# Raw weight blocks of Strassen units kept by rows and loaded in two row halves, instead of by column halves

## The chip, the cores and the metric

The kernel runs on one core of one Trainium2 chip. The metric is the device time of one execution, in microseconds (us), as the median over several runs. Five engines take part: TensorE (PE in the profile, its weight loads PEld), VectorE (DVE), ScalarE (ACT), GpSimd (POOL) and SyncE (SP), which here mainly starts transfers between device memory and on-chip memory. Each engine works through its own instructions in the order in which they stand in the built program, and waits at the first one whose inputs or whose place are not ready.

## The reference

One sequence of 512 tokens, with 16 learned positions ahead of it (528 rows), runs through two layers of width 1024: gated linear attention (GLA) and then differential softmax attention. Each layer is a norm, one wide input projection, the attention branch, a SiLU gate and an output projection. The changed lines serve the input projections alone:

```python
def gla_branch(xn, w_in, w_gate_up, b_gate, gnorm, w_out):
    proj = xn @ w_in                      # [528, 1024] @ [1024, 6160]
    q, k, v, z, g_lr = jnp.split(proj, ...)
...
def diff_branch(xn, w_in, lam_vecs, gnorm, w_out, rel_table, lambda_init):
    proj = xn @ w_in                      # [528, 1024] @ [1024, 8192]
    q, k, v, z = jnp.split(proj, 4, axis=-1)
```

All of it is float32.

## The kernel before

**Projections as Strassen units.** Float32 products are made of three passes over numbers split in a high and a low part (`split`: ACT writes the high part, line L269; DVE subtracts it from the source to get the low part, L270). On top of that, most projections are done by a Strassen-like scheme with seven products instead of eight. A *unit* is 256 columns of a weight matrix with all 1024 rows: a 2 by 2 arrangement of blocks, each of 512 rows and 128 columns. The kernel numbers them 0 to 3: 0 and 1 are the upper and the lower 512 rows of the first 128 columns, 2 and 3 the same of the second 128 columns. On chip a block is 128 partitions by 512 numbers (four groups of 128 rows, side by side). There are 45 such loads in the program; 41 of them are Strassen units (`want_unit`) and 4, the first ones of the GLA layer, are used without sums (`want_plain`).

**From raw block to operand.** `load_blocks` (L281) reserves one of two `raw` buffers of 1 MB each and starts two transfers from SP (L285), one for each column half: blocks 0 and 1, then blocks 2 and 3. Each transfer is 512 KB in 1024 pieces of 512 bytes. A unit then needs six parts, made in this order by `Weights.make_one`:

- `a11`: block 0 split (128x512);
- `sum`: three DVE additions (L337, helper `add`): `sum[1]` = block 2 + block 3, `sum[0]` = `sum[1]` + block 0, and block 2 += block 0 in place;
- `s21`: `sum` split (128x1024, tiles `wh` and `wl`);
- `a12`: block 1 split;
- `s43`: the *outer add* (`raw<-raw,sum`, a fourth addition), block 1 += `sum[0]` in place, and then blocks 1 and 2 split together (128x1024). This split's DVE half, `wl<-raw`, mostly is the last reader of the buffer, and releases it for the load after the next;
- `a22`: block 3 split.

**Orders.** PE's order is written by hand: `Unit.run` yields its products (L402, 128x264 matmuls, into the banks `bx`, `by` and `bv`), and a `Weaver` weaves them between the attention's own matmuls. The orders on DVE and ACT are not written down. The build's scheduler puts an instruction where it expects its inputs and its engine to be free, with some helpers (`partial` at L423, the combining adds `t`, `qs` at L448 to L452) at a raised priority. So a changed dependence between two instructions can change the order of others.

**What else stands around the change in the GLA layer.** For each head, a value block is normalised: ACT sums squares (L1215), DVE scales the sum (L512) and POOL takes a power (L513), ACT multiplies (L1217), PE transposes (L1239), DVE applies the gate (L1241). Output of a unit is evicted by L448 to L452.

Of the kernel before, what the change touches and what calls it, by code (L numbers as in the profile page):

```python
# [11 lines left out]
F32 = mybir.dt.float32  # L12
# [8 lines left out]
P = 128  # L21
# [52 lines left out]
class Weaver:  # L74
# [6 lines left out]
    def add(self, gen, us=0.0):  # L81
        self.queue.append(gen)
        self.left += us
        return gen
# [124 lines left out]
def trunk(ctx, tc, x, meta, g_norm, gla_w_in, gla_w_gate_up, gla_b_gate, gla_gnorm, gla_w_out,  # L209
# [3 lines left out]
    act, dve, pe, pool, sp = nc.scalar, nc.vector, nc.tensor, nc.gpsimd, nc.sync  # L213
# [8 lines left out]
    wp = ctx.enter_context(tc.tile_pool(name="wp", bufs=2))  # L222
# [8 lines left out]
    def T(p, shape, dt, tag, **kw):  # L231
        uid[0] += 1
        return p.tile(shape, dt, tag=tag, name=f"{tag}_{uid[0]}", **kw)
# [29 lines left out]
    def split(hi, lo, src, scale=None, keep=False):  # L263

        if keep:
            act.activation(hi, src, AF.Copy)
            kept.append(lambda: dve.tensor_tensor(lo, src, hi.bitcast(F32), op=ALU.subtract))
        elif scale is None:
            act.activation(hi, src, AF.Copy)  # L269
            dve.tensor_tensor(lo, src, hi.bitcast(F32), op=ALU.subtract)  # L270
        else:
            act.activation(hi, src, AF.Copy, scale=scale)
            dve.scalar_tensor_tensor(lo, src, scale, hi.bitcast(F32), op0=ALU.mult, op1=ALU.subtract)
# [4 lines left out]
        sp.dma_start(t, w[r0:r0 + nk * P, c0:c0 + ncol].rearrange("(k p) c -> p k c", p=P))  # L278
        return t

    def load_blocks(w, c0):  # L281

        t = T(wp, [P, 4, 512], F32, "raw")
        for i in range(2):
            sp.dma_start(t[:, 2 * i:2 * i + 2, :].rearrange("p j (k c) -> p (j k) c", k=4),  # L285
                         w[:, c0 + i * P:c0 + (i + 1) * P].rearrange("(k p) c -> p k c", p=P))
        return t

    W = Weaver()
    behind = W.behind  # L290

    def load(key):
        t = load_w(*key) if len(key) == 4 else load_blocks(*key)
        while behind:
            behind.pop(0)()
        return t

    def w_pair(shape):
        return [T(wp, shape, F32R, tag) for tag in ("wh", "wl")]
# [7 lines left out]
    ws = Weights(lambda *key: load(key), {"pair": 2, "sum": 1, "a11": 1, "a12": 1, "a22": 1})  # L307
# [8 lines left out]
    def behind_gate():  # L316
        st = ExitStack()
        for i in W.gated:
            st.enter_context(tc.issue_after(i.ins))
        return st  # L320

    def block_pair(src, keep=False):
        wh, wl = w_pair([P, 2, 512])
        split(wh, wl, src, keep=keep)
        return [[t[:, i, :] for t in (wh, wl)] for i in range(2)]

    def want_unit(w, c0, calm=False):
        def single(tag, b):
            def fn(raw):
                t = [T(wp, [P, 512], F32R, tag + part, bufs=1) for part in "hl"]  # L330
                with tc.issue_after(W.moved.ins) if calm and b == 0 else ExitStack():
                    split(*t, raw[:, b, :])
                return t
            return Part(tag, fn)

        def add(o, a, b):
            dve.tensor_tensor(o, a, b, op=ALU.add)  # L337

        def sums(raw):
            t = T(wp, [P, 2, 512], F32, "sum", bufs=1)  # L340
            add(t[:, 1, :], raw[:, 2, :], raw[:, 3, :])
            add(t[:, 0, :], t[:, 1, :], raw[:, 0, :])
            add(raw[:, 2, :], raw[:, 2, :], raw[:, 0, :])
            return t

        def outer(raw):
            add(raw[:, 1, :], raw[:, 1, :], su.t[:, 0, :])
            ws.room["sum"] += 1
            return block_pair(raw[:, 1:3, :])

        a11, a12, a22 = single("a11", 0), single("a12", 1), single("a22", 3)
        su = Part("sum", sums)
        s21 = Part("pair", lambda raw: block_pair(su.t))
        s43 = Part("pair", outer)
        ws.want((w, c0), [a11, su, s21, a12, s43, a22])
        return a11, a12, a22, s21, s43

    def want_plain(w, c0, keep=False):

        def first(raw):  # L360
            with behind_gate():
                return block_pair(raw[:, :2, :], keep)

        return ws.want((w, c0), [Part("pair", first),
                                 Part("pair", lambda raw: block_pair(raw[:, 2:, :]))])

    def mm3(ps, a, b, first=True, last=True, **kw):

# [240 lines left out]
    for b in range(5):  # L609
        t0, n = BLK[b]  # L610
        t = T(gp, [P, D], F32, ("qs", "ks")[b - 1]) if b in (1, 2) else {0: z2, 3: v2[0], 4: v2[1]}[b][:, 1, :]
# [5 lines left out]
    sp.dma_start(glr_raw, g_w_in[:, 6144:6160].rearrange("(k p) c -> p k c", p=P))  # L617

    v_first = [want_plain(g_w_in, 2048 + c, c == 0) for c in (0, 256)]
    ws.held = 1  # L620
    ws.fetch()
# [124 lines left out]
    for k0 in range(0, KT, 2):  # L746
        if k0 + 2 < KT:
            scaled_pair(k0 + 2)
        i, ks = k0 // 4, slice(k0 % 4, k0 % 4 + 2)
# [28 lines left out]
    def q_gla_qk(hd, s):  # L778
        c = 256 * hd
        us = [(want_unit if hd else want_plain)(g_w_in, c0) for c0 in (c, 1024 + c)]  # L780

        def factor_of(i, sign, e=None):
# [176 lines left out]
    for k in range(KT):  # L959
        for n in range(2):  # L960
            for i, x in enumerate((X["b11"], b12) if k < 4 else (X["b21"], X["b22"])):
                if k == 0:
                    warm_up((3, 3, 1, 4)[2 * n + i], idle)
                if (k, 2 * n + i) in turns_of:
                    b, half = turns_of[k, 2 * n + i]
# [49 lines left out]
    first = q_gla_qk(0, heads[0])  # L1015
# [395 lines left out]
    for i in range(2):  # L1411
        w = ws.take()
# [354 lines left out]
    for hd in range(D_HEADS):  # L1767
# [6 lines left out]
        keep = {D_HEADS - 1: 0.0, D_HEADS - 2: 22.0}.get(hd, 3.0)  # L1774
# [85 lines left out]
def build(shapes):  # L1860
    import concourse.bacc as bacc

    nc = bacc.Bacc("TRN2", target_bir_lowering=False, num_devices=1, dynamic_dma_scratch_size=512)
    args = [nc.dram_tensor(f"in_{n}_dram", shp, F32, kind="ExternalInput").ap() for n, shp in shapes]
    args.append(nc.dram_tensor("out_0_dram", (1, NR, D), F32, kind="ExternalOutput").ap())
    with tile.TileContext(nc) as tc:
        trunk(tc, *args)
    return nc
# [15 lines left out]
```

## Time and profile before

| what | value |
|---|---|
| median of the runs | 984.81 us (984.6 to 985.19) |
| the profiled execution's own time | 986.58 us |
| span of the profile (first to last instruction) | 984.8 us, granted PE clock 0.997 |
| PE busy | 969.7 us (98%) in 7065 matmuls |
| DVE busy | 777.3 us (79%) in 1584 instructions |
| ACT busy | 615.6 us (63%) in 1306 instructions |
| queue q1 (all plain transfers) | 147504 packets, 89.61 MB, 33.5% of 16 DMA engines |

The span leaves out 1.8 us of the execution's own time, which lie ahead of the first and behind the last instruction. The profiled execution is 1.8 us above the median of the runs. "Busy" says how long an engine had an instruction under way; a row of the timeline has the start, the duration, the engine, the line and the tiles (written tile, arrow, read tiles), and in brackets how long the engine had been idle and what ended that. A releaser given as "DMA raw" is the landing of a weight transfer.

### The profile page before, as it was taken

To read this page: it belongs to the slowest core of one execution; us is meant where nothing else is said; L and a number is where in the kernel's file an instruction comes from. 1 tells how busy PE (TensorE), PEld (TensorE's weight loads), DVE (VectorE), ACT (ScalarE), POOL (GpSimd) and SP (SyncE) were. 2 spreads that over 40 slices of the span, in tenths; PEclk is the share of its full clock that TensorE was granted. 3 is DMA by queue.
4 is the path that set the end of the run, shared out by engine and by line. 5 is a ranking of instruction groups with operands and counts; after the bars stand their busy time and mean duration, and the time that the engine had idled before them with its cause. 6 is when DMAs were issued, how large, how long until landed. Compare 5 with 4: busy or idle time off the path is not lost. (4 is left out here: it accounts for less than half of the span.)

```text
span 984.8 us, 18186 instructions
## 1 busy us (share of the span) xinstructions
PE 969.7 (98%) x7065; PEld 915.2 (93%) x7065; DVE 777.3 (79%) x1584; ACT 615.6 (63%) x1306; POOL 50.7 (5%) x68
## 2 busy tenths in 40 slices
PE   8999999999999999999999999999999999999997
PEld 8999999999999999999999998898998999988896
DVE  7889985987687888556998885877968879677785
ACT  7776755566546666536657675566764667654583
POOL 1000000000000100000000101001010000000001
PEclk9999999999999999999999999999999999999999
DMA  7322223731363322122332524335353351622222
GB/s 194 87 74 74 74 87 127 143 87 44 111 158 87 86 73 76 68 86 87 97 87 77 149 63 137 83 98 135 86 147 86 97 135 49 184 60 81 86 65 86
DMA packets 150474, 96.27 MB, mean 98 GB/s; under 512 B 33117, under 2 KB 136829, under 8 KB 150384
## 3 DMA queue, kind: packets, MB, share of 16 engines
q1 hardware_dynamic: 147504, 89.61, 33.5%
q10 hardware_dynamic: 2880, 5.46, 1.6%
q8 instruction: 57, 0.93, 0.4%
q14 instruction: 33, 0.27, 0.1%
HBM read 83.64 MB, written 7.57 MB: 93 GB/s over the span
## 5 line engine op out<-in xcount | busy, mean ns | idle before, releaser
L270 DVE TENSOR_TENSOR wl<-raw,wh 128x1024 fp32r<-128x1024 f32 x98 | 119.6, 1222 | 26.9 <-ACT wh L269 19.9
L269 ACT ACTIVATE wh<-raw 128x1024 fp32r<-128x1024 f32 x98 | 103.0, 1053 | 52.2 <-PE by L938 26.6
L402 PE MATMUL bv<-x,wh 128*128 128x264 f32 (+1 forms) x656 | 97.7, 287 | 0.8 <-DVE t L448 0.6
L402 PE MATMUL bx<-x,wh 128*128 128x264 f32 (+1 forms) x640 | 95.1, 286 | 0.2
L402 PEld LDWEIGHTS bv<-x,wh 128*128 128x128 f32 x656 | 86.3, 189 | 1.8 <-DVE t L448 1.5
L402 PEld LDWEIGHTS bx<-x,wh 128*128 128x128 f32 x640 | 84.6, 188 | 1.4 <-ACT u L423 0.6
L392 PE MATMUL bx<-x,wh 128*128 128x512 f32 (+1 forms) x256 | 62.5, 386 | 0.0
L423 ACT ACTIVATE u<-bx 128x264 f32<-128x264 f32 (+1 forms) x120 | 45.4, 379 | 24.1 <-PE bx L402 21.9
L270 DVE TENSOR_TENSOR wl<-sum,wh 128x1024 fp32r<-128x1024 f32 x41 | 50.1, 1221 | 11.0 <-ACT wh L269 9.7
L1618 ACT ACTIVATE p<-p,st 128x528 f32<-128x528 f32 (+3 forms) x64 | 36.4, 569 | 31.7 <-DVE st L1616 31.4
L402 PE MATMUL bv<-x,wl 128*128 128x264 f32 (+1 forms) x328 | 55.2, 285 | 0.1
L1654 POOL TENSOR_TENSOR st<-st,mhalf 128x1 f32<-128x1 f32 x32 | 30.6, 957 | 466.4 <-ACT on L1652 422.8
L402 PE MATMUL bx<-x,wl 128*128 128x264 f32 (+1 forms) x320 | 53.8, 285 | 0.0
L392 PEld LDWEIGHTS bx<-x,wh 128*128 128x128 f32 x256 | 44.5, 188 | 8.0
L269 ACT ACTIVATE wh<-sum 128x1024 fp32r<-128x1024 f32 x41 | 43.3, 1055 | 10.7 <-PE bv L402 4.0
L269 ACT ACTIVATE a11h<-raw 128x512 fp32r<-128x512 f32 x41 | 25.7, 628 | 35.5 <-DMA raw<-in_diff_w_in_dram 18.0
L402 PE MATMUL by<-x,a12h 128*128 128x264 f32 (+1 forms) x320 | 46.7, 286 | 0.2 <-DVE t L448 0.2
L402 PE MATMUL bx<-x,a11h 128*128 128x264 f32 (+1 forms) x320 | 46.5, 285 | 0.0
L402 PEld LDWEIGHTS bv<-x,wl 128*128 128x128 f32 x328 | 45.9, 188 | 0.4 <-issue 0.3
L402 PEld LDWEIGHTS bx<-x,wl 128*128 128x128 f32 x320 | 45.0, 188 | 0.5 <-DVE wl L270 0.2
L402 PEld LDWEIGHTS bx<-x,a11h 128*128 128x128 f32 x320 | 42.3, 188 | 0.8
L402 PEld LDWEIGHTS by<-x,a12h 128*128 128x128 f32 x320 | 41.7, 188 | 0.6 <-DVE t L448 0.4
(479 smaller groups left out, 2644.2 us busy)
## 6 DMA issues: line engine op xcount, KB each, us to landing
raw<-in_gla_w_in_dram SPq DMA_DIRECT2D x48, 512.0 KB, 4.2
raw<-in_diff_w_in_dram SPq DMA_DIRECT2D x42, 512.0 KB, 5.6
raw<-in_diff_w_in_dram SPq DMA_DIRECT2D x11, 1024.0 KB, 5.7
raw<-in_gla_w_out_dram SPq DMA_DIRECT2D x8, 1024.0 KB, 5.3
raw<-in_diff_w_out_dram SPq DMA_DIRECT2D x8, 1024.0 KB
vd<-planes ACTq DMA_DIRECT2D x12, 268.0 KB, 3.0
vd<-keep ACTq DMA_DIRECT2D x8, 264.0 KB, 2.3
T<-bdr SPq DMA_DIRECT2D x8, 264.0 KB, 3.6
```

The costliest lines, as they stand in the source:

```text
L269: act.activation(hi, src, AF.Copy)
L270: dve.tensor_tensor(lo, src, hi.bitcast(F32), op=ALU.subtract)
L392: pe.matmul(bank, a[:, k, :], b[k] if n0 is None else b[k][:, n0 + i * nn:n0 + (i + 1) * nn], start=n == 0 and ks[0] == 0, stop=n == len(t ...
L402: pe.matmul(bank[:, :x[q].shape[2]], w[p][:, k * P:(k + 1) * P], x[q][:, k, :], start=first and i == 0, stop=i == len(PASSES) - 1, skip_gr ...
L423: W.moved = act.activation(t, self.bx[:, :self.n], AF.Copy, scale=self.sc)
L1618: act.activation(p[:, :nk], p[:, :nk], AF.Exp, scale=-1.0, bias=st[:, m:m + 1], accum_out=st[:, 2 + m:3 + m])
L1654: pool.tensor_tensor(ms, ms, mhalf[:, :1], op=ALU.pow)
```

## The change

The raw tile becomes 128 partitions by 8 row groups by 256 columns. For the 41 Strassen units the two transfers now bring row halves: first the upper 512 rows (blocks 0 and 2), then the lower (blocks 1 and 3). A transfer is still 512 KB, now in 512 pieces of 1 KB. The four plain loads keep their column halves (`by_cols`). Every block is now a strided view, four runs of 128 numbers with 256 between their starts, and so the splits and additions of a unit read or write such views; `sum` and the split operands stay contiguous. The outer add has another place to write to: `block 0 = block 1 + sum[0]`, so that blocks 0 and 2, which lie side by side in the upper row groups, are the pair that is split last. (Block 0's other readers are `a11`'s split and the second and third addition; block 1's is `a12`'s split.)

```diff
-    def load_blocks(w, c0):
+    def load_blocks(w, c0, by_cols=False):
-        t = T(wp, [P, 4, 512], F32, "raw")
-        for i in range(2):
-            sp.dma_start(t[:, 2 * i:2 * i + 2, :].rearrange("p j (k c) -> p (j k) c", k=4),
-                         w[:, c0 + i * P:c0 + (i + 1) * P].rearrange("(k p) c -> p k c", p=P))
+        t = T(wp, [P, 8, 2 * P], F32, "raw")
+        if by_cols:
+            t = t.rearrange("p k (i c) -> p (k i) c", c=P)
+            for i in range(2):
+                sp.dma_start(t[:, 8 * i:8 * i + 8, :],
+                             w[:, c0 + i * P:c0 + (i + 1) * P].rearrange("(k p) c -> p k c", p=P))
+            return t
+        for j in range(2):
+            sp.dma_start(t[:, 4 * j:4 * j + 4, :],
+                         w[512 * j:512 * j + 512, c0:c0 + 2 * P].rearrange("(k p) c -> p k c", p=P))
         return t
+
+    def block(raw, b):
+        i, j = divmod(b, 2)
+        return raw[:, 4 * j:4 * j + 4, i * P:(i + 1) * P]
+
+    def in_rows(t):
+        return t.rearrange("p (k c) -> p k c", c=P)
...
     def block_pair(src, keep=False):
         wh, wl = w_pair([P, 2, 512])
-        split(wh, wl, src, keep=keep)
+        if src.shape[1] == 2:
+            split(wh, wl, src, keep=keep)
+        elif src.shape[1] == 8:
+            split(*[t.rearrange("p i (k c) -> p (i k) c", c=P) for t in (wh, wl)], src, keep=keep)
+        else:
+            split(*[t.rearrange("p i (k c) -> p i k c", c=P) for t in (wh, wl)],
+                  src.rearrange("p k (i c) -> p i k c", c=P), keep=keep)
...
-                    split(*t, raw[:, b, :])
+                    split(*[in_rows(o) for o in t], block(raw, b))
...
-            add(t[:, 1, :], raw[:, 2, :], raw[:, 3, :])
-            add(t[:, 0, :], t[:, 1, :], raw[:, 0, :])
-            add(raw[:, 2, :], raw[:, 2, :], raw[:, 0, :])
+            add(in_rows(t[:, 1, :]), block(raw, 2), block(raw, 3))
+            add(in_rows(t[:, 0, :]), in_rows(t[:, 1, :]), block(raw, 0))
+            add(block(raw, 2), block(raw, 2), block(raw, 0))
...
         def outer(raw):
-            add(raw[:, 1, :], raw[:, 1, :], su.t[:, 0, :])
+            add(block(raw, 0), block(raw, 1), in_rows(su.t[:, 0, :]))
             ws.room["sum"] += 1
-            return block_pair(raw[:, 1:3, :])
+            return block_pair(raw[:, :4, :])
...
-        return ws.want((w, c0), [Part("pair", first),
-                                 Part("pair", lambda raw: block_pair(raw[:, 2:, :]))])
+        return ws.want((w, c0, True), [Part("pair", first),
+                                       Part("pair", lambda raw: block_pair(raw[:, 8:, :]))])
```

The numbers of instructions on PE, ACT, DVE, POOL and SP stay as they are, and so do PE's, POOL's and SP's orders. On DVE the scheduler now puts the outer add earlier in nearly all units (it no longer has to stand behind `a12`'s split), and a few others move with it; lines behind the change stand 19 further down (L448 becomes L467, L512 becomes L531, L1241 becomes L1260).

The first place that the prediction speaks of is DVE in the second GLA head's value block (head 1, counted from 0), around 213 us of the trace of before. `raw_5233` and `raw_5391` are two units in turn, `t_5434` evicts a product, `st_5551` is the scaled sum of squares of the 16 learned rows. Before:

```order
L270 TENSOR_TENSOR a22l_5524<-raw_5233,a22h_5523 128x512
L450 TENSOR_TENSOR t_5434<-bv_5437,u_5419 128x264
L270 TENSOR_TENSOR wl_5520<-raw_5233,wh_5519 128x1024
L512 TENSOR_SCALAR st_5551<-st_5551 16x1
L903 SCALAR_TENSOR_TENSOR z_5278<-t_5502,t_5435 128x528
```

And with the change:

```order
L270 TENSOR_TENSOR a22l_5524<-raw_5233,a22h_5523 128x512
L469 TENSOR_TENSOR t_5434<-bv_5437,u_5419 128x264
L356 TENSOR_TENSOR raw_5391<-raw_5391,sum_5531 128x4x128
L270 TENSOR_TENSOR wl_5520<-raw_5233,wh_5519 128x1024
L531 TENSOR_SCALAR st_5551<-st_5551 16x1
L922 SCALAR_TENSOR_TENSOR z_5278<-t_5502,t_5435 128x528
```

The outer add of `raw_5391` now stands ahead of `wl_5520`, which releases the buffer of `raw_5233` for the next load, and ahead of `st_5551`. In the third head (head 2) the same happens ahead of `wl_6796`.

The second place is DVE in the same head, some 7 us later: `raw_5577` is the unit that is loaded into the buffer released by `wl_5520`, `qs_5580` evicts products of the unit under way, `t_5673` is the gate (L1241) and `st_5686` the scaled sum of squares of the second row block. Before:

```order
L337 TENSOR_TENSOR raw_5391<-raw_5391,sum_5531 128x512
L448 SCALAR_TENSOR_TENSOR qs_5580<-bv_5582,u_5637 128x264
L337 TENSOR_TENSOR sum_5723<-raw_5577 128x512
L270 TENSOR_TENSOR a11l_5720<-raw_5577,a11h_5719 128x512
L337 TENSOR_TENSOR sum_5723<-sum_5723,raw_5577 128x512
L337 TENSOR_TENSOR raw_5577<-raw_5577 128x512
L448 SCALAR_TENSOR_TENSOR qs_5580<-by_5655,u_5637 128x264
L1241 TENSOR_TENSOR t_5673<-ps_5668,z_5278 128x512
L270 TENSOR_TENSOR a22l_5713<-raw_5391,a22h_5712 128x512
L270 TENSOR_TENSOR y_1039_5607<-t_5673,y_1038_5606 128x4x128
L512 TENSOR_SCALAR st_5686<-st_5686 128x1
```

And with the change:

```order
L356 TENSOR_TENSOR sum_5723<-raw_5577 128x512
L467 SCALAR_TENSOR_TENSOR qs_5580<-bv_5582,u_5637 128x264
L356 TENSOR_TENSOR sum_5723<-sum_5723,raw_5577 128x512
L270 TENSOR_TENSOR a11l_5720<-raw_5577,a11h_5719 128x512
L356 TENSOR_TENSOR raw_5577<-raw_5577 128x4x128
L467 SCALAR_TENSOR_TENSOR qs_5580<-by_5655,u_5637 128x264
L270 TENSOR_TENSOR a22l_5713<-raw_5391,a22h_5712 128x512
L1260 TENSOR_TENSOR t_5673<-ps_5668,z_5278 128x512
L356 TENSOR_TENSOR raw_5577<-raw_5577,sum_5723 128x4x128
L270 TENSOR_TENSOR y_1039_5607<-t_5673,y_1038_5606 128x4x128
L531 TENSOR_SCALAR st_5686<-st_5686 128x1
```

The first addition, which waits for the load of `raw_5577`, now stands ahead of an eviction that stood before it; `a22l_5713` moved ahead of the gate `t_5673`, and the outer add of `raw_5577` came in behind the gate.

More of the change, by code (lines that the diff above doesn't have):

```diff
@@ L361, in first @@
             with behind_gate():
-                return block_pair(raw[:, :2, :], keep)
-        return ws.want((w, c0), [Part("pair", first),
-                                 Part("pair", lambda raw: block_pair(raw[:, 2:, :]))])
+                return block_pair(raw[:, :8, :], keep)
+        return ws.want((w, c0, True), [Part("pair", first),
+                                       Part("pair", lambda raw: block_pair(raw[:, 8:, :]))])
     def mm3(ps, a, b, first=True, last=True, **kw):
```

## The prediction

> **What bounds the kernel now.** I read the page first, then busy time by stretch, then the waits.
>
> ```profile
> PE 969.7 (98%) x7065; PEld 915.2 (93%) x7065; DVE 777.3 (79%) x1584; ACT 615.6 (63%) x1306; POOL 50.7 (5%) x68
> core 0: us, PE busy (x) PEld busy (x) DVE busy (x) ACT busy (x) POOL busy (x), PEclk, DMA share, GB/s
> 0.00:16.00 16.00, 13.47 (x87) 12.68 (x88) 10.39 (x30) 10.40 (x20) 3.19 (x10) 0.89 0.91 256
> 301.00:306.00 5.00, 4.44 (x37) 4.22 (x36) 3.80 (x8) 1.94 (x5) 0.00 (x0) 1.00 0.01 2
> 306.00:330.00 24.00, 23.63 (x181) 22.53 (x181) 19.78 (x35) 16.34 (x32) 1.53 (x2) 1.00 0.33 88
> 361.00:368.00 7.00, 6.15 (x49) 5.47 (x49) 6.78 (x17) 3.79 (x12) 0.00 (x0) 1.00 0.16 40
> 368.00:799.00 431.00, 430.67 (x3081) 405.00 (x3080) 336.13 (x706) 271.67 (x596) 25.79 (x25) 1.00 0.35 99
> 799.00:802.00 3.00, 2.87 (x24) 2.66 (x24) 2.21 (x5) 2.84 (x9) 0.00 (x0) 1.00 0.78 175
> 900.00:916.00 16.00, 15.15 (x103) 13.40 (x103) 11.77 (x24) 9.62 (x27) 1.34 (x2) 1.00 0.28 80
> 977.00:985.00 8.00, 1.19 (x11) 0.98 (x9) 2.97 (x7) 2.35 (x7) 0.55 (x1) 0.78 0.30 114
> ```
>
> PE sets the time: it is busy 969.7 of 984.8 us at full granted clock, and its instructions and their order stay as they are. So the change can only move PE's idle time, 15.1 us. Of that the start (16.00 − 13.47 = 2.5 us, a stage with the plain loads) and the tail (8.00 − 1.19 = 6.8 us, behind the last unit) have no changed load. The body keeps 15.1 − 2.5 − 6.8 = 5.8 us. In the 431 us from 368 to 799 PE is idle 0.33 us in all: whatever the loads do there, nothing can be gained, only lost. The stretches with idle time worth naming are 301 to 306 (0.56), 306 to 330 (0.37), 361 to 368 (0.85), 799 to 802 (0.13) and 900 to 916 (0.85).
>
> What do these wait for? The loads reach PE by DVE:
>
> ```profile
> L337 DVE TENSOR_TENSOR sum<-raw 128x512 f32<-128x512 f32 x41 | 28.2, 687 | 13.5 <-DMA raw<-in_gla_w_in_dram 8.3 <-DMA raw<-in_diff_w_in_dram 5.2
> 302.20 0.69 DVE L337 TENSOR_TENSOR sum<-raw 128x512 f32<-128x512 f32 x1 [1.92 <-DMA raw<-in_gla_w_in_dram]
> 302.81 0.43 DVE L448 SCALAR_TENSOR_TENSOR t<-bv,u 128x264 f32<-128x264 f32 x1
> 303.29 0.88 PE L402 MATMUL bv<-x,wh 128*128 128x264 f32 x5 [0.56 <-DVE t L448]
> 360.02 0.69 DVE L337 TENSOR_TENSOR sum<-raw 128x512 f32<-128x512 f32 x1 [0.60 <-DMA raw<-in_gla_w_in_dram]
> 903.10 0.69 DVE L337 TENSOR_TENSOR sum<-raw 128x512 f32<-128x512 f32 x1 [3.39 <-DMA raw<-in_diff_w_in_dram]
> ```
>
> The first addition of a unit is the only DVE instruction that a landing holds up: 13.5 us over 41 units. Most of it costs PE nothing. At 302.20 it does: the eviction L448 stands behind the waiting addition, and PE, which needs the bank, is idle 0.56 us at 303.29. The idle time from 361 and from 900 on follows DVE queues that began with such a wait (0.60 and 3.39 us).
>
> **What earlier landing is worth.** Transfer sizes and counts stay, pieces double to 1 KB. The kernel already has loads of both kinds, at 150 GB/s in windows of 7 us, 1 MB each: the first window holds a pair in 512-byte pieces, the second a single 1 MB load in pieces of 1 KB.
>
> ```profile
> 561.80:568.80 7.00, 7.00 (x60) 7.00 (x59) 6.88 (x19) 6.21 (x13) 0.00 (x0) 1.00 0.55 150
> 434.00:441.00 7.00, 7.00 (x60) 6.98 (x59) 4.34 (x9) 2.91 (x4) 0.00 (x0) 1.00 0.48 150
> L278 SPq DMA_DIRECT2D raw<-in_diff_w_in_dram x11: 367/368/368, 434.0 to 883.2; - x11
> DMA to landing us min/median/max: 5.3/5.5/5.7
> 897.09 0.99 SPq L285 DMA_DIRECT2D raw<-in_diff_w_in_dram  x2
> ```
>
> The DMA engines are busy 0.07 × 7 = 0.49 us less for a megabyte. That is the upper bound of what a unit gains. The lower is zero: the single load of 1 KB pieces takes 5.5 us to land, and the pair issued at 897.09 has landed by 903.10, 6.0 us later, of which 0.99 − 0.37 = 0.62 us is the issue of the second transfer, which stays. So landing time hardly follows the piece size; I take 0.15 us, nearer to the landing rows than to the busy share, because what is waited for is a landing. Applied to the five stretches, each capped by its idle time: 4 × 0.15 + 0.13 = 0.7, less 0.1, since I could not follow the idle time of 900 to 916 to a load in full: **−0.6 us**. Bounds: 0, and 0.49 three times plus 0.37 and 0.13, −2.0 us.
>
> The Trainium skill, in "DMA: Bandwidth & Descriptors", section "Why small descriptors are slow (HBM only)", gives every packet a fixed overhead of about 3 cycles beside one for each 32 bytes; by that two packets of 512 bytes cost 38 cycles, one of 1 KB 35, an estimate of 8% less. The busy shares above fall by 13%, so the trace agrees in direction; whether a landing follows is the rival below.
>
> **What the blocks cost as strided views.** No run of 128 with 256 between starts is read by an addition in the trace, but the splits of `load_w` tiles read just such views (`raw[:, :, ca:ca + ncol]`):
>
> ```profile
> L270 DVE TENSOR_TENSOR wl<-raw,wh x9: 1217/1225/1226, 432.8 to 485.0; 128x1024 fp32r<-128x1024 f32 x9
> L270 DVE TENSOR_TENSOR wl<-raw,wh 128x1024 fp32r<-128x1024 f32 x98 | 119.6, 1222 | 26.9 <-ACT wh L269 19.9 <-PE bx L392 6.5 <-PE by L392 0.2
> ```
>
> The strided ones (432.8 to 485.0) take 1225 ns, the mean over all 98, contiguous ones included, is 1222. So I take 0, bounded by 3 ns per instruction below and, for views in four dimensions (`s43`) and strided writes that no row shows, 20 ns, an estimate of some seven times that difference: 41 units × 8 DVE instructions (four additions, four low parts) × 0.02 = 7 us of DVE time, covered where DVE has 21% to spare. Without cover, in the five stretches, it would be 5 × 8 × 0.02 = 0.8 us.
>
> `a12` (block 1) now comes with the second transfer. Its split stands well behind the first addition, which needed both transfers before as now: 0.
>
> **What the moved additions cost.** An outer add takes 0.61 us from start to start (220.21 to 220.82 below). It is neither more nor less work, but it now stands ahead of things that are waited for. Of the places I followed, two are on PE's path.
>
> ```profile
> 213.34 0.43 DVE L450 TENSOR_TENSOR t<-bv,u 128x264 f32<-128x264 f32 x1
> 213.69 1.22 DVE L270 TENSOR_TENSOR wl<-raw,wh 128x1024 fp32r<-128x1024 f32 x1
> 214.93 0.99 SPq L285 DMA_DIRECT2D raw<-in_gla_w_in_dram  x2
> 215.12 0.14 DVE L512 TENSOR_SCALAR st<-st 16x1 f32<-16x1 f32 x1 [0.22 <-ACT t L1215]
> 215.35 0.54 POOL L513 TENSOR_TENSOR st<-st,mhalf 16x1 f32<-16x1 f32 x1 [79.87 <-DVE st L512]
> 215.92 0.68 ACT L1217 ACTIVATE t<-ps,st 16x512 f32<-16x512 f32 x1
> 216.65 0.41 PE L1239 MATMUL ps<-ident,t 16*128 16x16 f32 x4 [0.22 <-ACT t L1217]
> 220.21 0.69 DVE L337 TENSOR_TENSOR raw<-raw,sum 128x512 f32<-128x512 f32 x1
> 220.82 0.43 DVE L448 SCALAR_TENSOR_TENSOR qs<-bv,u 128x264 f32<-128x264 f32 x1
> 221.88 0.69 DVE L337 TENSOR_TENSOR sum<-raw 128x512 f32<-128x512 f32 x1 [0.63 <-DMA raw<-in_gla_w_in_dram]
> 224.40 0.43 DVE L448 SCALAR_TENSOR_TENSOR qs<-by,u 128x264 f32<-128x264 f32 x1
> 224.75 0.68 DVE L1241 TENSOR_TENSOR t<-ps,z 128x512 f32<-128x512 f32 x1
> 226.77 0.15 DVE L512 TENSOR_SCALAR st<-st 128x1 f32<-128x1 f32 x1
> 228.33 0.66 PE L1239 MATMUL ps<-ident,t 128*128 128x128 f32 x4
> ```
>
> *Head 1, first.* The outer add goes in at 213.69. The split `wl` starts 0.61 later, the 0.22 us of idle ahead of L512 absorb a part, the landing that started this queue is 0.15 earlier: L512 at 215.12 is 0.61 − 0.22 − 0.15 = 0.24 late. The chain behind it, L512, POOL, ACT L1217, PE at 216.65, has no slack, since PE already waits 0.22 there: **+0.24 us**.
>
> *Head 1, second.* SP issues the next load at 214.93, at the end of that split; it is 0.61 − 0.15 = 0.46 late, the landing 0.46 − 0.15 = 0.31. So `sum` starts at 222.19. Then the order of the second place in the change's section: between `sum` and the gate L1241 stand one eviction more (0.35, from 224.40 to 224.75) and `a22l` (0.60), which makes the gate 0.31 + 0.95 = 1.26 late; behind it the outer add takes the place of `a22l`, and L512 at 226.77 is 1.26 late too. L513 and L1217 follow, and PE's transposes at 228.33 run out just in time now. If the landing is again 6.85 us behind its issue (214.93 to 221.78), PE waits some 1.2 us; if it takes the 6.0 us of the pair at 897.09, 0.85 less, 0.4. I take **+0.7 us**. Bounds 0 and +1.3.
>
> *Head 2* is the same pattern ahead of the split at 317.90:
>
> ```profile
> 317.90 1.22 DVE L270 TENSOR_TENSOR wl<-raw,wh 128x1024 fp32r<-128x1024 f32 x1
> 320.86 0.42 PE L1239 MATMUL ps<-ident,t 16*128 16x16 f32 x4 [0.21 <-ACT t L1217]
> 326.79 0.69 DVE L270 TENSOR_TENSOR a11l<-raw,a11h 128x512 fp32r<-128x512 f32 x1 [0.74 <-ACT a11h L269]
> ```
>
> +0.24 by the same working at 320.86. Its second part is eased by the 0.74 us that DVE stands idle at 326.79, which the addition moved ahead can fill: 0.95 − 0.74 = 0.2. Together **+0.45 us**.
>
> The other moved additions go into DVE queues with slack, or leave queues (in front of `s21`'s split) that PE does not wait for. From 368 to 799 there is nothing to win; for some unlucky place I add **+0.1** (0 to +1).
>
> Sum: −0.6 + 0.24 + 0.7 + 0.45 + 0.1 = **+0.9 us**. Against the profiled execution's 986.58 that makes 987.5; that execution lies 1.8 us above the median of the runs, so the median goes from 984.81 to 985.7.
>
> **Rivals.**
> 1. *Landings follow the pieces.* Each landing comes 0.49 us sooner, the stretches give 2.0 us back, and the queues of the two heads, which begin with waits for a landing, come early enough to take the 0.61 us of the outer add almost whole: 984.8 − 2.0 = 982.8, and 982.0 if the wait at 900 to 916 goes altogether. For it: the busy shares. Against it: 5.5 us for a load of 1 KB pieces. (This is what the packet overhead of "DMA: Bandwidth & Descriptors" in the Trainium skill would do, if transfers were bound by it.)
> 2. *The waiting addition becomes the gate.* The first `sum` now stands ahead of evictions in heads 1 and 2, and an in-order DVE that waits for a late landing holds `qs`, the gate and L512 together. Full price: 1.26 in each head, 0.46 at each of the two first places (no help from landings), and again 0.6 at one more head where the scheduler's moves end on the path: 1.26 × 2 + 0.46 × 2 + 0.6 = 4.0, so 988.8 us. It decides from the point where landings are not earlier than now. For it: 6.85 us for the load at 214.93. Against: 0.74 us of idle time in head 2, and not all evictions are urgent.
> 3. *Nothing reaches PE*: landings and moves are both covered, 984.8 us. For it: 98% busy.
>
> **How the numbers follow.** A measurement of this kernel tells no change from one of some 0.2%, 2 us. My forecast, 985.7, has 0.42, and rival 3, which lies within the same 2 us, 0.08. Rival 1 has 0.20, rival 2 with the unseen cost of views 0.30. So: faster 0.20, within 0.2% 0.50, slower 0.30. The range goes from rival 1's 982.8 to 988.4, just short of rival 2's full price; bounds of the terms (−2.0 and +0.24 + 1.3 + 0.45 + 1 + 0.8 = +3.8) lie about there.
>
> **What would show it.** Right: idle time ahead of `sum` from landings is about 12 us of the 13.5; PE's wait for L1217's result at the 216 and 320 places grows by 0.2 to 0.3; the transposes of 228 wait 0.4 to 1.2; additions still at 687 ns and splits at 1222. Wrong: landing times of pairs down by half a microsecond with less than 10 us of such idle time (rival 1), or PE idle above 17 us with its waits on evictions L467 to L471 (rival 2), or additions above 700 ns, which would make DVE the cause.

## The result and the profile after

The changed kernel takes 983.74 us (median of 22 runs, 983.07 to 985.28) against 985.02 us for the kernel before in the same runs (984.32 to 986.45): a ratio of 0.9986, 95% interval 0.9979 to 0.9992, so 1.3 us or 0.14% faster. The prediction had said 985.7 us, 0.9 us slower. The profiled execution took 984.03 us, its span is 982.3 us.

The page's first row and the busy time by stretch, with the columns and the stretches of the prediction:

```profile
PE 967.6 (99%) x7065; PEld 914.7 (93%) x7065; DVE 777.2 (79%) x1584; ACT 616.2 (63%) x1306; POOL 50.8 (5%) x68
0.00:16.00 16.00, 14.14 (x94) 12.91 (x95) 10.81 (x31) 11.13 (x21) 3.43 (x11) 1.00 0.89 254
301.00:306.00 5.00, 5.00 (x43) 5.00 (x42) 4.71 (x9) 2.80 (x5) 0.00 (x0) 1.00 0.00 0
361.00:368.00 7.00, 6.51 (x57) 6.27 (x56) 6.78 (x17) 4.88 (x13) 0.00 (x0) 1.00 0.47 152
368.00:799.00 431.00, 429.86 (x3069) 403.81 (x3068) 335.19 (x704) 270.04 (x591) 26.90 (x25) 1.00 0.32 98
```

Around 302 and 362 us idle time of PE is gone (0.56 to 0, 0.85 to 0.49 us), and in the long second layer, where the prediction said that one could only lose, it grew from 0.33 to 1.14 us. The start of the two profiles differs too (2.53 us idle before, 1.86 now), though nothing there was changed; in the kernels below it varies by up to 1.6 us, and so everything that follows is counted from 20 us on.

PE runs the same 7065 matmuls in the same order in every kernel of this study; only their times differ. That makes the best reading of all: the start of a matmul in one profile less the start of the same matmul in the profile of before. This table, worked out from the traces, shows that difference in us at eleven places, with the value at 20 us taken off (negative: earlier than before). The two profiles of the changed kernel lie up to 0.6 us apart in it, so single values are no better than that:

```
at us of the kernel before    92   100   211   240   300   370   676   690   700   900   976
the change                 -0.21 +0.69 +0.51 +0.38 +0.68 -1.71 -1.55 -1.14 -0.49 -0.87 -1.81
the change, second profile -0.09 +0.85 +0.65 +0.16 +0.15 -1.87 -1.73 -0.91 -0.29 -0.51 -1.23
order alone                +0.06 +0.99 +0.79 +2.69 +3.07 +3.42 +3.85 +3.81 +4.47 +4.67 +4.51
columns into rows          -0.03 +0.91 +0.85 +2.07 +2.52 +2.95 +3.39 +3.39 +4.01 +3.97 +3.70
outer add behind a12       -0.21 -0.21 -0.20 -0.99 -1.47 -2.93 -2.95 -2.45 -2.45 -2.37 -3.13
the same, columns          +0.03 +0.03 +0.03 +0.13 +0.67 +0.26 +0.47 +0.43 +0.44 +1.00 +0.91
one transfer               +0.36 +1.31 +1.11 +0.45 +1.05 +0.44 +0.63 +1.89 +2.52 +3.76 +3.88
```

(The rows below the first two are the experiments.) The change loses 0.9 us between 92 and 100 and 1.1 to 1.4 us from 676 to 700, and gains 2.0 to 2.4 us between 300 and 370 and 0.7 to 0.9 us behind 900. It is a sum of two large terms, not of small ones. ACT's order moved as well as DVE's: going by the two traces, 66 of its 1306 places hold another instruction.

The gain begins at the landings. The grouped row of the first additions, and the landing times of the transfers (the last number of an issue row is the median from issue to landing, over the transfers whose landing the trace has; the 48 hold the 8 unchanged plain ones). First the issue rows of before, then the rows of the changed kernel:

```profile
raw<-in_gla_w_in_dram SPq DMA_DIRECT2D x48, 512.0 KB, 4.2
raw<-in_diff_w_in_dram SPq DMA_DIRECT2D x42, 512.0 KB, 5.6
```

```profile
L356 DVE TENSOR_TENSOR sum<-raw 128x512 f32<-128x512 f32 x41 | 28.1, 686 | 9.1 <-DMA raw<-in_gla_w_in_dram 5.7 <-DMA raw<-in_diff_w_in_dram 3.1
raw<-in_gla_w_in_dram SPq DMA_DIRECT2D x48, 512.0 KB, 3.9
raw<-in_diff_w_in_dram SPq DMA_DIRECT2D x42, 512.0 KB, 4.6
```

DVE's waits for landings went from 13.5 to 8.8 us (5.7 + 3.1), and the additions take as long as before (686 against 687 ns).

The loss, in the timelines of DVE and PE, at the place of the table's first loss. Before:

```profile
93.34 0.43 DVE L450 TENSOR_TENSOR z<-bv,u 128x264 f32<-128x264 f32 x1
93.69 0.68 DVE L270 TENSOR_TENSOR a<-t,a 128x512 fp32r<-128x512 f32 x1
94.22 0.89 PE L402 MATMUL bv<-x,wh 128*128 128x264 f32 x6
```

And with the change, with PE's wait at the transposes of 228 in the last row:

```profile
92.38 0.69 DVE L356 TENSOR_TENSOR raw<-raw,sum 128x512 f32<-128x512 f32 x1
92.99 0.68 DVE L270 TENSOR_TENSOR a<-t,a 128x512 fp32r<-128x512 f32 x1
93.59 0.43 DVE L469 TENSOR_TENSOR z<-bv,u 128x264 f32<-128x264 f32 x1
94.07 0.99 PE L421 MATMUL bv<-x,wh 128*128 128x264 f32 x6 [0.63 <-DVE z L469]
227.98 0.66 PE L1258 MATMUL ps<-ident,t 128*128 128x128 f32 x4 [0.35 <-ACT t L1236]
```

An outer add of head 1's first unit, and with it the split `a<-t,a`, now stands ahead of the eviction L469 that frees bank `bv`, and PE, which did not wait there before, is idle for 0.63 us until it is done. The prediction had not looked at this place. At 227.98 PE waits 0.35 us for the chain of the transposes, as its second term had it.

### The profile page after: what moved, and what is told of

The parts are those of the page before. It is cut to its first block, busy times and chain, and to the rows that moved or that the text cites. A ratio compares the mean times of both kernels' runs of the same rounds, so it can differ in the third digit from the quotient of the medians.

```text
span 982.3 us, 18166 instructions
## 1 busy us (share of the span) xinstructions
PE 967.6 (99%) x7065; PEld 914.7 (93%) x7065; DVE 777.2 (79%) x1584; ACT 616.2 (63%) x1306; POOL 50.8 (5%) x68
## 5 line engine op out<-in xcount | busy, mean ns | idle before, releaser
L269 ACT ACTIVATE wh<-raw 128x1024 fp32r<-128x1024 f32 x98 | 103.1, 1054 | 54.1 <-PE by L957 26.5
L269 ACT ACTIVATE wh<-sum 128x1024 fp32r<-128x1024 f32 x41 | 43.2, 1054 | 12.3 <-PE bv L421 4.1
L269 ACT ACTIVATE a11h<-raw 128x512 fp32r<-128x512 f32 x41 | 25.8, 628 | 31.1 <-DMA raw<-in_diff_w_in_dram 15.8
```

## The experiments

Every ratio is to the kernel before, measured beside it on the same chip, with its 95% interval. (On these chips the kernel before took 986.0 to 986.4 us.)

### The order alone

The kernel before, with one thing of the change: the outer add writes block 0, and the pair is blocks 0 and 2. Loads and blocks are as before.

```diff
-            add(raw[:, 1, :], raw[:, 1, :], su.t[:, 0, :])
+            add(raw[:, 0, :], raw[:, 1, :], su.t[:, 0, :])
             ws.room["sum"] += 1
-            return block_pair(raw[:, 1:3, :])
+            return block_pair(raw.rearrange("p (i j) c -> p j i c", j=2)[:, 0])
```

> The kernel before, loads of 512-byte pieces by column halves and contiguous blocks, with one thing of the change: the outer add writes block 0, and blocks 0 and 2 are the pair. So only the order on DVE and ACT moves. Theory: the new stall at 94 us and those near 228, 243 and 692 us appear, nothing is gained near 302, 316, 362 and 900, and the kernel is 1 to 2 us slower than before (ratio 1.001 to 1.002). Rival (the freed order is what makes the change faster): 983 to 984, ratio 0.998 to 0.9995.

989.87 us, ratio 1.0038 (1.0024 to 1.0052): 3.7 us slower, about twice the top of what was expected. PE's waits in the timeline of this kernel (line numbers of the kernel before):

```profile
94.50 0.99 PE L402 MATMUL bv<-x,wh 128*128 128x264 f32 x6 [0.65 <-DVE z L450]
217.46 0.41 PE L1239 MATMUL ps<-ident,t 16*128 16x16 f32 x4 [0.51 <-ACT t L1217]
230.38 0.66 PE L1239 MATMUL ps<-ident,t 128*128 128x128 f32 x4 [1.25 <-ACT t L1217]
```

The stall at 94 is here without any change of a load. The wait at 216.65, 0.22 before, is 0.51 now: 0.29 more. The transposes of 228 wait 1.25 us. So the freed order is a loss by itself, and the rival that it is what makes the kernel faster has fallen.

### Column halves into the strided tile

The changed kernel, with its views and its outer add, loaded as before. By the traces its order on PE, DVE, ACT and POOL is that of the order alone in every place; the changed kernel's differs from it in 18 of DVE's 1584 places and 32 of ACT's 1306.

```diff
-        for j in range(2):
-            sp.dma_start(t[:, 4 * j:4 * j + 4, :],
-                         w[512 * j:512 * j + 512, c0:c0 + 2 * P].rearrange("(k p) c -> p k c", p=P))
+        for i in range(2):
+            sp.dma_start(t[:, :, i * P:(i + 1) * P],
+                         w[:, c0 + i * P:c0 + (i + 1) * P].rearrange("(k p) c -> p k c", p=P))
```

> The changed kernel's tile, views and outer add, but loaded as before: two column halves in 512-byte pieces, written into the strided places. Against the changed kernel only the pieces and the blocks that come first differ; against the run of the order alone only the strided views differ. Theory: the gains near 302, 316, 362 and 900 us go, the new stalls stay, time as the run of the order alone, 985.5 to 987, additions still at 685 ns. Rival (strided views cost): additions or splits on raw are slower by 20 ns or more and the time is 1 us or more above that of the order alone. Rival (blocks 0 and 1 first is better for a12): ACT's waits for a12 near 173, 278, 545, 671 and 799 us go and the time is below 985.

989.6 us, ratio 1.0036 (1.0022 to 1.005). Against the order alone only the strided views are new, and the two ratios agree: the views cost nothing that can be measured. Against the changed kernel (0.9986) the row halves with their larger pieces are missing, and those few places that the scheduler moved for them: together they are worth 1.0036 − 0.9986 = 0.5%, 4.9 us, give or take 1.5 by the two intervals. The first addition, the outer add, and the time from issue to landing of the changed line's transfers, in this kernel:

```profile
L356 DVE TENSOR_TENSOR sum<-raw 128x512 f32<-128x512 f32 x41 | 28.2, 687 | 18.3 <-DMA raw<-in_gla_w_in_dram 12.7 <-DMA raw<-in_diff_w_in_dram 5.5
L356 DVE TENSOR_TENSOR raw<-raw,sum 128x512 f32<-128x512 f32 x41 | 28.1, 686 | 0.4
DMA to landing us min/median/max: 4.1/4.6/5.6
```

and the last row again in the profile of the changed kernel:

```profile
DMA to landing us min/median/max: 3.6/4.0/5.4
```

The trace has a landing for 11 of the 82 transfers, the same 11 in both. Their median is 0.6 us lower in 1 KB pieces than in pieces of 512 bytes, their mean 0.5 us (4.3 against 4.8). What the addition waits for is the unit's second transfer: the four recorded ones land 5.0 to 5.3 us after the unit's first issue in the changed kernel, 5.8 to 6.1 us here. And in the eight units in which DVE waits for the landing in both profiles, the addition starts 0.5 us sooner after the first issue in the mean (from 0.25 us later to 1.3 us sooner). With the changed order and old loads DVE waits 18.2 us for landings; with the new loads it waits half of that. The rival that column halves serve `a12` better did not show in the time.

### The outer add put back

The changed kernel, with one ordering edge: the outer add stands behind `a12`'s low split on DVE, as it had to before.

```diff
-            add(block(raw, 0), block(raw, 1), in_rows(su.t[:, 0, :]))
+            with tc.issue_after(a12.low.ins):
+                add(block(raw, 0), block(raw, 1), in_rows(su.t[:, 0, :]))
```

> The changed kernel, with the outer add put back behind a12's low split on DVE (one ordering edge). Loads, pieces and views are those of the changed kernel. Theory (earlier landings give about 2.5 us, moved outer adds take about 1.5 us back): the stalls that came new with the change at 94 us (bank bv waits for an eviction behind the outer add, 0.6 us), near 228 and 243 us go, the gains near 302, 316 and 362 stay, and the time is 982 to 983, ratio to before 0.997 to 0.998. Rival (the order of the additions is worth nothing, the net gain is all there is): 983.5 to 984, ratio 0.9985 to 0.999.

982.75 us, ratio 0.9967 (0.9955 to 0.9979). In the first layer the order of DVE is that of before again but for four small moves (near 61, 114, 178 and 382 us); in the second the scheduler still places many instructions otherwise. The two places of the losses, in the timelines:

```profile
92.32 0.43 DVE L471 TENSOR_TENSOR z<-bv,u 128x264 f32<-128x264 f32 x1
93.22 0.89 PE L423 MATMUL bv<-x,wh 128*128 128x264 f32 x6
226.71 0.60 PE L1260 MATMUL ps<-ident,t 128*128 128x128 f32 x4
```

No wait is left at either. Of the change's loss from 676 to 700, the part behind 690 is gone with the edge too, the part before it is not (table); the last experiment looks at that. The kernel with the edge takes 3.4 us less than the kernel before on the same chip. Since this kernel beats both, it was run once more beside the changed kernel on one chip:

> The changed kernel itself, on the chip of the run beside it and against the kernel before: ratio 0.998 to 0.9992 as recorded, PE's step at 94 us and those at 680 and 692 again there, 0.3 to 0.5% below the same order with column halves.

> The run with the outer add behind a12 in all units again, beside the changed kernel on the same chip. Theory: 1.2 to 2.2 us below the changed kernel, ratio to before 0.9955 to 0.998. Rival: no more than 0.5 us below it, so that the earlier difference was one of chips.

The changed kernel took 984.63 us, ratio 0.9986 (0.9977 to 0.9995), the same ratio as above; the kernel with the edge 982.41 us, ratio 0.9965 (0.9951 to 0.9978): 2.2 us below it, the top of what was expected.

### One unit alone

The edge of the run before, in the one unit whose outer add stands ahead of the eviction at 93 us.

```diff
-            with tc.issue_after(a12.low.ins):
+            with tc.issue_after(a12.low.ins) if w is g_w_in and c0 == 256 else ExitStack():
```

> The changed kernel, with the outer add put back behind a12's low split in one unit alone, the first one of head 1 (columns 256 of the query part), whose outer add stands ahead of the eviction of bank bv at 93 us. Theory (the price of a moved outer add is the wait of PE for what stands behind it): PE's step at 94 us against the kernel before (0.8 us) goes, all other steps stay, and the time is 0.7 to 0.9 us below the changed kernel of the same call. Rival (the bank is late for another reason, or PE catches the time up later): the step stays, or it comes back within 20 us, and the times agree within 0.3 us.

983.87 us, ratio 0.9978 (0.9969 to 0.9987), 0.76 us below the changed kernel on the same chip. PE's times against that kernel's step by −0.77 us at 94 and stay lower to the end (−0.70 at the last matmul). One addition of 0.61 us in the wrong place of a queue, with the split that went ahead with it, cost the kernel three quarters of a microsecond; nothing later took it up.

### The edge, with column halves

Both edits together: the outer add behind `a12`, and column halves in 512-byte pieces into the strided tile.

> The run with the outer add behind a12, but loaded by column halves in 512-byte pieces into the strided tile. Neither the pieces nor, in the first layer, the order of the additions differ from the kernel before; strided views and the place of the sum do. Theory (gain is all from landings, loss all from the order): 0.1% of the kernel before, from 0.3% faster to equal in the second layer's order, so ratio 0.998 to 1.001, and 0.3 to 0.5% slower than with row halves. Rival (the order of the edge itself is better than both): ratio 0.9975 or less.

987.41 us, ratio 1.0012 (1.0003 to 1.0021), just above the range that was expected; the table's row shows its losses of 0.5 us between 240 and 300 and between 700 and 900, whose cause stays open. Against the same kernel with row halves (0.9967) it is 0.45% slower, with 18 places of DVE and 32 of ACT moved here too. So the row halves are worth 4.9 us with the new order and 4.4 us with the old one, each to about 1.5 us.

### One transfer, and four

The changed kernel with one transfer of 1 MB per unit, and the kernel with the edge with four of 256 KB, all in pieces of 1 KB.

```diff
-        for j in range(2):
-            sp.dma_start(t[:, 4 * j:4 * j + 4, :],
-                         w[512 * j:512 * j + 512, c0:c0 + 2 * P].rearrange("(k p) c -> p k c", p=P))
+        sp.dma_start(t, w[:, c0:c0 + 2 * P].rearrange("(k p) c -> p k c", p=P))
...
+        for j in range(4):
+            sp.dma_start(t[:, 2 * j:2 * j + 2, :],
+                         w[256 * j:256 * j + 256, c0:c0 + 2 * P].rearrange("(k p) c -> p k c", p=P))
```

> The changed kernel, with a single transfer of 1 MB in 1 KB pieces per unit instead of two row halves. The second half can land no later than now if the issue of a second transfer costs something, while a11 has to wait for the whole megabyte. Theory (landing of the last byte is what PE waits for, and it follows the pieces): the first additions start within 0.2 us of where the changed kernel has them, a11 lands 1.3 us later, time 983.5 to 985. Rival (it is the split in two transfers that lands early): the additions that wait for landings start 0.4 us or more later, and the time is above 985.

> The run with the outer add behind a12, with four transfers of 256 KB (two row groups each, 1 KB pieces) instead of two of 512 KB. Theory (the last byte of a unit is bound by the engines' time for its pieces, which stays): additions that wait for landings start within 0.3 us of the two-transfer run, and the issues, 0.4 us each on SP, make the last landing a little later: time 982.5 to 985, ratio 0.9965 to 0.999. Rival (more transfers under way land sooner, as two did against one): the waits of sum for landings shrink by another 0.3 us each and the ratio is below 0.996.

One transfer: 990.04 us, ratio 1.0039 (1.0025 to 1.0053), a time above 985 as the rival had it. Four: 987.07 us, ratio 1.0012 (1.0003 to 1.0021), worse by 0.45% than the two transfers of that kernel, and worse than both expectations. These times are not the transfers' alone: with one transfer the scheduler filled 125 of DVE's 1584 and 60 of ACT's 1306 places otherwise than in the changed kernel, with four 16 and 2 otherwise than with the edge. The landings are seen in two units, near 308 and 897 us: when SP begins to issue (queue SP, with the time until the last issue is done), and when the first addition starts that waited for the landing. First the pair in 512-byte pieces, in the run with columns into rows:

```profile
309.63 0.99 SPq L291 DMA_DIRECT2D raw<-in_gla_w_in_dram  x2
315.54 0.69 DVE L356 TENSOR_TENSOR sum<-raw 128x512 f32<-128x512 f32 x1 [1.97 <-DMA raw<-in_gla_w_in_dram]
900.30 0.99 SPq L291 DMA_DIRECT2D raw<-in_diff_w_in_dram  x2
906.36 0.69 DVE L356 TENSOR_TENSOR sum<-raw 128x512 f32<-128x512 f32 x1 [3.44 <-DMA raw<-in_diff_w_in_dram]
```

The pair in 1 KB pieces, in the changed kernel:

```profile
307.39 0.92 SPq L291 DMA_DIRECT2D raw<-in_gla_w_in_dram  x2
312.75 0.69 DVE L356 TENSOR_TENSOR sum<-raw 128x512 f32<-128x512 f32 x1 [1.43 <-DMA raw<-in_gla_w_in_dram]
895.49 0.92 SPq L291 DMA_DIRECT2D raw<-in_diff_w_in_dram  x2
900.88 0.69 DVE L356 TENSOR_TENSOR sum<-raw 128x512 f32<-128x512 f32 x1 [2.76 <-DMA raw<-in_diff_w_in_dram]
```

One transfer:

```profile
307.88 0.37 SPq L290 DMA_DIRECT2D raw<-in_gla_w_in_dram  x1
313.53 0.69 DVE L354 TENSOR_TENSOR sum<-raw 128x512 f32<-128x512 f32 x1 [1.71 <-DMA raw<-in_gla_w_in_dram]
900.19 0.37 SPq L290 DMA_DIRECT2D raw<-in_diff_w_in_dram  x1
906.61 0.69 DVE L354 TENSOR_TENSOR sum<-raw 128x512 f32<-128x512 f32 x1 [3.79 <-DMA raw<-in_diff_w_in_dram]
```

Four:

```profile
308.07 1.90 SPq L291 DMA_DIRECT2D raw<-in_gla_w_in_dram  x4
313.90 0.69 DVE L357 TENSOR_TENSOR sum<-raw 128x512 f32<-128x512 f32 x1 [1.29 <-DMA raw<-in_gla_w_in_dram]
897.75 1.91 SPq L291 DMA_DIRECT2D raw<-in_diff_w_in_dram  x4
903.63 0.69 DVE L357 TENSOR_TENSOR sum<-raw 128x512 f32<-128x512 f32 x1 [3.25 <-DMA raw<-in_diff_w_in_dram]
```

From the first issue to the addition a unit takes 5.9 and 6.1 us as a pair of 512-byte pieces, 5.4 and 5.4 as a pair of 1 KB pieces, 5.7 and 6.4 as one transfer, 5.8 and 5.9 as four. The pair in 1 KB pieces is the best in these two, but they are not typical. Over the eight units in which DVE waits in both profiles, one transfer is 0.2 us later than the pair of the changed kernel in the mean (from 1.0 sooner to 1.0 later); four are 0.2 and 0.5 us later in the mean than the two profiles of the kernel with the edge (six and five units). So the rival's 0.4 us or more is not shown. The single transfer is still 0.4 us sooner than the pair in 512-byte pieces (mean of 13 units): the earlier landing goes with the larger pieces, and not with the division into row halves. The single transfer also brings `a11` no sooner than the last byte. How the 5 us that it costs divide between landings, `a11` and the moved order stays open.

### One a12, later

The kernel with the edge, and one ACT instruction moved: the high part of `a12` of the unit that lands near 670 us goes behind two small copies.

```diff
+                gate = W.moved if calm and b == 0 else W.third if b == 1 and w is d_w_in and c0 == 3 * DI + 256 * 4 else None
-                with tc.issue_after(W.moved.ins) if calm and b == 0 else ExitStack():
+                with tc.issue_after(gate.ins) if gate else ExitStack():
...
-        act.activation(dst[96 - lo:128 - lo], src, AF.Copy, **kw)
+        W.third = act.activation(dst[96 - lo:128 - lo], src, AF.Copy, **kw)
```

> The run with the outer add behind a12, and one ACT instruction moved: the high part of a12 of the unit whose load lands at 669 us (head 4 of the second layer, z columns) stands behind the two small copies am instead of ahead of them. In the changed kernel this a12 holds ACT 0.5 us for the second transfer, and PE is 0.4 us late at L1680 near 680. Theory (block 1 coming with the second transfer costs where its split stands ahead of urgent copies): the 0.4 us near 680 go and nothing else moves, 0.3 to 0.4 us below the run without it, about the limit of what the medians tell. Rival (the late chain there is POOL's or the eviction's): the step in PE's times near 680 stays at 0.4.

982.89 us, ratio 0.9962 (0.9949 to 0.9975): the median tells nothing from the run without it. The trace does. ACT and PE in the changed kernel:

```profile
670.69 0.63 ACT L269 ACTIVATE a12h<-raw 128x512 fp32r<-128x512 f32 x1 [0.48 <-DMA raw<-in_diff_w_in_dram]
671.22 0.26 ACT L269 ACTIVATE aT<-ps 128x128 fp32r<-128x128 f32 x1
680.78 0.44 PE L1680 MATMUL ps<-ident,on 128*128 128x128 f32 x2 [0.68 <-ACT on L1674]
```

and here:

```profile
669.62 0.27 ACT L269 ACTIVATE aT<-ps 128x128 fp32r<-128x128 f32 x1
670.57 0.63 ACT L269 ACTIVATE a12h<-raw 128x512 fp32r<-128x512 f32 x1 [0.27 <-DMA raw<-in_diff_w_in_dram]
679.86 0.44 PE L1683 MATMUL ps<-ident,on 128*128 128x128 f32 x2 [0.24 <-ACT on L1677]
```

The copy `aT` no longer stands behind a split that waits for the second transfer, and PE's wait at that transpose falls from 0.68 to 0.24 us; against the kernel with the edge, whose wait there was alike (0.78), PE's times step by −0.52 us. Elsewhere (near 79 and 241 us, where the two kernels have the same order) the two profiles part by 0.5 and 0.7 us in the other direction, and so the time of the whole kernel can't show it.

## Why the prediction was wrong

The measured time lies in the range, but the sign was wrong: both of the sum's large terms were too small, and the landings' more so. That the time lay so near the forecast (1.3 us down against 0.9 us up) is luck: two terms of some 4 us nearly cancel.

- **PE sets the time, and only its idle time can move:** right. All kernels run the same matmuls, and the table accounts for the ratios: −1.2 and −1.8 us for the change (0.9986, −1.4), +4.5 for the order alone (+3.7), −3.1 for the edge (−3.2).
- **Earlier landing, −0.6 us: the step that failed.** Each landing was to be 0.15 us sooner. Measured is 0.5 us in the mean of the eight units, and in time 4.4 to 4.9 us. Two readings went wrong. Between the pair's 6.0 us and the 5.5 us of a single load in 1 KB pieces lay the answer, and the prediction explained it away: 0.62 us of the pair was "the issue of the second transfer, which stays". The issue stays (0.92 us for a pair), but it runs while the first transfer is under way (none of these landed in under 3.6 us), and the pair in 1 KB pieces takes 5.4 us in that unit with it. The upper bound, 0.49 us from the engines' busy share, is the size that was measured. Second, the gain was capped by the idle time that the kernel before had. It is larger, since an earlier landing also pays for part of the new order: in the table the new order alone has lost 3.4 us by 370, with early landings the same order has gained 1.7 to 1.9.
- **Strided views at nothing:** right, 1.0036 against 1.0038 with the same order on all engines, first additions 686 to 687 ns in the kernel before, the changed one and the one with column halves.
- **`a12` with the second transfer at nothing:** right but for one place that was tested, 0.4 to 0.5 us near 680. It asked only whether the split stands behind the addition that waits on DVE; on ACT it stands alone, ahead of copies that PE waits for. DVE's waits were in fact the smaller part: ACT's splits in L269 sat idle 27.6 us for weight landings in the kernel before, and 24.4 in the changed one.
- **The outer add in head 1, first, +0.24:** right for the order alone (+0.29). With the early landings the sign turned: PE no longer waits at that transpose and is 0.4 us further ahead by 217.
- **In head 1, second, +0.7, bounds 0 to 1.3:** the mechanism was there. PE's transposes wait 1.25 us in the order alone (the full price of 1.26 was worked out), and 0.35 in the change, where the load is earlier: half the term.
- **Head 2, +0.45:** with the order alone it is about +0.3 from 300 to 370; in the change nothing of it is left. The working there also left out the later load (0.31) that it had counted in head 1.
- **Other moved additions, +0.1 (0 to +1):** mis-sized. The order alone loses 0.9 us at 94, 0.4 us at 243 and some 1.3 us from 370 to 900. "DVE queues with slack" was said of places that had not been checked against what stands behind the addition; at 94 it is a bank's eviction.
- **Rival 1** (0.49 us sooner, a chance of 0.20) named the mechanism that decided, though it let the new order cost almost nothing; its sign came in, landings half a microsecond sooner with less than 10 us of idle time (8.8). **Rival 2** is near what the new order costs with the old loads: +4.0 us, against +3.7 for the order alone. That is partly luck, for it laid 3.4 us on heads 1 and 2, where the table gives 2.6 (from 211 to 370), and the rest was lost in other places.

## What to carry to other kernels

When the pieces of a load change, compare times from issue to landing as a whole, and don't subtract an issue that runs beside the transfer; the engines' busy time was the better guide here. A dependence that is taken away lets a scheduler move an instruction up, and a place where that puts it ahead of an eviction or a short copy that TensorE waits for can cost its full length or more (0.77 us for an addition of 0.61 at 94, but 0.29 at 217); list what stands behind it at each place before calling it slack. Here holding the old place with one edge kept the gain and gave back the loss: 0.9965 against 0.9986.

## What the runs showed of the hardware

- A transfer of 512 KB from these weights lands in a median of 4.0 us in pieces of 1 KB and 4.6 us in pieces of 512 bytes (means 4.3 and 4.8; 11 recorded landings each, two transfers issued one behind the other). The mean time of a 512-byte packet was 30.1 ns in the kernel before, that of a 1 KB packet 52.1 ns in the changed one: 13% less for a kilobyte. The Trainium skill, in "DMA: Bandwidth & Descriptors", section "Why small descriptors are slow (HBM only)", names a fixed overhead per packet, by which 8% was the estimate; the 13% measured agree in direction.
- The first addition starts 0.5 us sooner after the unit's first issue with the pair in 1 KB pieces than with the pair in 512-byte pieces (mean of eight units). One transfer of 1 MB in 1 KB pieces was 0.2 us later than the pair, four of 256 KB 0.2 to 0.5 us.
- Splits and additions on blocks of four runs of 128 numbers take as long as on contiguous ones, also when they write such views: outer additions have a median of 691 ns in the kernel before and 683 in the changed one, the 128x1024 splits of raw tiles on DVE 1225 and 1224.
